# Two groups of block 0's down products by Strassen's scheme, and a scheduler that holds 16-bit products for each other

## The chip, the cores and the metric

The kernel runs on one core of a Trainium2 chip. The metric is the device time of one execution in microseconds (us). The engines are named as in the profile: PE is TensorE (matmuls), DVE is VectorE, ACT is ScalarE, POOL is GpSimd, SP is SyncE, which issues the DMAs.

## The reference

One layer of an encoder, for 2048 prompt frames and 64 frames of a running stream, 1024 channels wide. Its second half, where most of the change lies, is a gated feed-forward network (FFN):

```python
x = x + jnp.concatenate([o_delta, o_pool], axis=-1) @ w_out
h = rmsnorm(x, norm2_w)
x = x + (jax.nn.silu(h @ w_gate) * (h @ w_up)) @ w_down
```

The first half makes `o_delta`, by a gated delta rule over chunks of frames for four heads, and `o_pool`, by means over trailing windows, from one input projection.

## The kernel before, in words

**Two stages.** The first stage (0 to about 940 us) runs over four blocks of 512 frames (the first has the 64 stream frames too). Its large products, the input and output projections, are fp32r matmuls (tiles `pp`, `pz`, weights `wsp`), each done three times on operands that are split into a high and a low part. Between them stand the small products of the delta rule: 16-bit ones (`py`, `pt`, `px` and `pf` with `_p` in their names, which solve the triangular system step by step), and plain fp32 ones and transposes (`pk`, `po`, `gr`, `ptv`). The delta rule is a chain: each small product waits for ACT or DVE to copy out the one before.

The second stage is the FFN. Its 2112 frames are cut into three blocks (`b` = 0, 1, 2) of two halves of 352 columns each. The 2816 hidden channels are 22 tiles `f`, in six groups of 4, 4, 4, 4, 2, 4 (`FGROUPS`, numbered `gi` = 0 to 5).

**Gate and up** (`gate_up`, L1530). For each f, the pair of gate and up products over the two halves of the input channels is done by Strassen's scheme in the Winograd form: seven products of 12 matmuls in place of eight (PSUM tiles `px`, `py`, `pz`). The seven weight forms are `11`, `12`, `22` and the sums `S1` to `S4`. In block 0 POOL makes these sums (`wrS`), DVE and ACT split them, and they are stored to DRAM; blocks 1 and 2 load them back (`prep_strassen`, L590). The result, `hr`, is silu(gate) * up for one f.

**Down, plain** (`down`, L1577). For a group, each of 8 output tiles and each half sums 12 matmuls over four f into a PSUM tile `d`, and DVE adds it to `y`. Each `hr` must first be split into a high and a low part (tile `h`).

**Down, Strassen** (`down_strassen`, L1611, with `factors`, L1588, and `prep_down`, L624). Two f make a pair. `factors` makes seven forms of a pair (tile `hq`, sums `q` on POOL, splits on ACT and DVE). `prep_down` makes the seven weight forms for two output tiles (sums `wrda`, `wrdb` on POOL, splits `wsd`, `wsdS`). Then four steps of seven products of 6 matmuls (PSUM tiles `dx`, `dy`, `dz`) are each added to one `y`. `plain` (L512) says which groups go which way: all of block 0, and the last group of block 2, are plain; the others go by Strassen.

**Memory that ties steps together.** The split `h` of block 0 lie in six slots of two buffers with the tag `op` (`six`, L1633); the factors `hq` and the split tiles `h3l` of a last plain group use the same two buffers. `hr` has three buffers.

**What sets the order.** `order` (L516 on) lists gate-up steps `gu` and down groups `dn`: a group stands behind the gate-up step after its last f, and group 0 (`LATER`) one step later still. Weights are prepared three sets ahead (`AHEAD`). All engine calls are recorded, and `Machine.issue` (L185) then puts each engine's instructions in an order by a model of their costs. For TensorE, `pick` (L283) chooses among the ready products. Kind `r` is fp32r, all others are small. When the last product was fp32r and there are other fp32r products ready, a small product is held back until `HOLD` us after it became ready (three numbers at L1692: for boosted ones, the others, and boosted ones before a given point of the program), so that several run together.

Of the kernel before, what the change touches and what calls it, by code (L numbers as in the profile page):

```python
# [25 lines left out]
NF = 22  # L26
# [18 lines left out]
SUBS2 = ((0, N2), (N2, N2))  # L45
FGROUPS = (4, 4, 4, 4, 2, 4)

SDOWN = (1, 2)
LASTPOOLS = {3: ((0,), (1,), (2, 3))}

FW = ("11", "S1", "S2", "12", "S3", "S4", "22")
# [8 lines left out]
class Machine:  # L60
# [124 lines left out]
    def issue(self):  # L185

        ops, self.ops = self.ops, []
        wait = {e: [] for e in self.free}
        ready = {e: [] for e in self.free}
        for op in ops:  # L190
            op.left = sum(1 for p in op.preds.values() if p.start is None)
            op.start = None

        def free(op):

            for nm in op.tiles:
                if not self.tiles[nm][1]:
                    self.parked.setdefault(nm, []).append(op)
                    return serve(self.tiles[nm][0])
            heapq.heappush(wait[op.eng], (op.ready, op.order, op))  # L200

        def serve(tag):

            q = self.queue[tag]
            nm = next((nm for nm in (q if tag[1] == "mm" else list(q)[:1]) if nm in self.parked), None)
            if nm and self.slots[tag]:
                q.remove(nm)
                at, self.tiles[nm][1] = heapq.heappop(self.slots[tag]), True
                for op in self.parked.pop(nm):
                    op.ready = max(op.ready, at)  # L210
                    free(op)
                serve(tag)

        for op in ops:
            op.left = 0
            for p in op.preds.values():
                if p.start is None:
                    op.left += 1
                    p.succs.append(op)
                else:  # L220
                    op.ready = max(op.ready, self.done(p, op))

        for op in ops:
            if op.eng == "sync" and op.succs and not op.store:
                op.rank = max(op.order, min(q.order for q in op.succs))
        for op in ops:
            if not op.left:
                free(op)
        out, front = [], 0
        while len(out) < len(ops):  # L230
            best = None
            for e in self.free:
                if ready[e]:
                    t = self.free[e]
                    if e == "sync":

                        t = max(t, self.wire - (BACKLOG if ready[e][0][0] < front + AHEAD_OPS else IDLE))
                        if wait[e]:
                            t = min(t, max(self.free[e], wait[e][0][0]))
                elif wait[e]:  # L240
                    t = max(self.free[e], wait[e][0][0])
                else:
                    continue
                if best is None or t < best[0]:
                    best = (t, e)
            t, e = best
            while wait[e] and wait[e][0][0] <= t:
                op = heapq.heappop(wait[e])[2]
                heapq.heappush(ready[e], (op.rank, op.order, op))
            if e == "sync" and self.wire - (BACKLOG if ready[e][0][0] < front + AHEAD_OPS else IDLE) > t:  # L250
                continue
            if e == "tensor":
                op = self.pick(ready[e], t)
                front = max(front, op.order)
            else:
                op = heapq.heappop(ready[e])[2]
            self.run(op, t)
            out.append(op)
            for nm in op.tiles:
                t = self.tiles[nm]  # L260
                t[2] -= 1
                t[3] = max(t[3], op.start + op.lat + 0.04)
                if not t[2]:
                    heapq.heappush(self.slots[t[0]], t[3])
                    serve(t[0])
                self.early -= t[4]
                self.gone = max(self.gone, t[3] if t[4] else 0.0)
            if not self.early and self.later:
                later, self.later = self.later, {}
                for tag, n in later.items():  # L270
                    self.slots[tag] = [self.gone] * n
                    serve(tag)
            for q in op.succs:
                q.ready = max(q.ready, self.done(op, q))
                q.left -= 1
                if not q.left:
                    free(q)
        for op in out:
            name, args, kw = op.call
            getattr(getattr(self.nc, op.eng), name)(*args, **kw)  # L280
            op.call = op.preds = op.succs = None

    def pick(self, ready, t):  # L283

        others = sorted(x for x in ready if x[2].kind != "r")
        if others:
            first = others[0]
            held = self.last == "r" and len(others) < len(ready) and t < min(x[2].ready + self.hold(x) for x in others)
            if held:
                first = min(x for x in ready if x[2].kind == "r")  # L290
            ready.remove(first)
            heapq.heapify(ready)
            return first[2]
        return heapq.heappop(ready)[2]
# [67 lines left out]
def hybrid_kernel(ctx, tc, a, o):  # L362
# [140 lines left out]
    groups, f0 = [], 0  # L503
# [6 lines left out]
        return ((0,), (1,)) if (b, gi) == (NB2 - 1, len(groups) - 1) else ((0, 1),)  # L510

    def plain(b, gi):  # L512
        return b not in SDOWN or len(halves(b, gi)) > 1

    order = []
    for b in range(NB2):  # L516
        for f in range(NF):
            order.append(("gu", b, f))
            order += [("dn", b, gi) for gi, (f0, G) in enumerate(groups) if f == min(f0 + G + LATER * (gi == 0), NF - 1)]
    for op in order:  # L520
        if op[0] == "gu":
            plan.append(("gu", op[2]))
# [1007 lines left out]
    def gate_up(b, f):  # L1530
        w = weights("gu", f)
        tag = f"{b}_{f}"
        raw = f2.tile([P, 2, N2], F32, tag="hr", name=f"hr{tag}", bufs=3)

        def add(ps, nw, nh, first=False):

            for i, t in enumerate(hq[nh]):
                ks = slice(i * P, (i + 1) * P)
                for q, (wi, ai) in enumerate(((0, 0), (0, 1), (1, 0))):
                    mm(ps, w[nw][:, wi, ks], t[:, ai, :], start=first and i == q == 0, stop=i == 3 and q == 2,  # L1540
                       skip_group_check=not first)
                pump()

        def sigmoid(e, x):
            act(e, x, AF.Exp, scale=-1.0)
            act(e, e, AF.Ln, bias=onec)
            act(e, e, AF.Exp, scale=-1.0)

        def finish(i, g, u):
            e = raw[:, i]  # L1550
            tt(e, e, g, ALU.mult)
            tt(e, e, u, ALU.mult)
            if b not in SDOWN:
                split(h3t[f % 6], slice(i * N2, (i + 1) * N2), e)


        x, y, z = (psg(f"p{i}_{tag}")[:, :N2] for i in "xyz")
        add(x, "11", "11", True)
        hurry(nc.scalar.copy, g1 := tmp(f"g1_{tag}"), x)
        add(y, "S1", "T1", True)  # L1560
        hurry(nc.scalar.copy, u2 := tmp(f"u2_{tag}"), y)
        add(x, "S2", "T2")
        hurry(nc.scalar.copy, g2 := tmp(f"g2_{tag}"), x)
        add(z, "12", "21", True)
        hurry(tt, g1, z, g1, ALU.add)
        sigmoid(raw[:, 0], g1)
        add(x, "S3", "T3")
        hurry(tt, u2, x, u2, ALU.add)
        add(y, "S4", "22")
        hurry(tt, g2, y, g2, ALU.add)  # L1570
        sigmoid(raw[:, 1], g2)
        finish(1, g2, u2)
        add(x, "22", "T4")
        finish(0, g1, x)
        return raw if b in SDOWN else h3t[f % 6]

    def down(b, gi, h3, ys, which, done):  # L1577
        f0, G = groups[gi]
# [66 lines left out]
    for op in order:  # L1645
        b = op[1]
        if op[0] == "gu":
# [3 lines left out]
            if op == ("gu", 0, 2):  # L1651
                nxt = Chain(between(-1))
            h3[f] = gate_up(b, f)
            if b in SDOWN:
                gi = max(g for g, (f0, G) in enumerate(groups) if f0 <= f)
                if plain(b, gi):
                    if f == groups[gi][0] or f == groups[gi][0] + 2:
                        two = opool.tile([P, 2, 2, TB2], F32R, tag="op", name=f"h3l{f}", bufs=2)
                    for i in range(2):
                        split(two[:, f % 2], slice(i * N2, (i + 1) * N2), h3[f][:, i])  # L1660
                    h3[f] = two[:, f % 2]
                elif f % 2:
                    machine.boost = HURRY if f == NF - 1 else 0
                    h3[f] = factors(b, f, h3.pop(f - 1), h3[f])
                    machine.boost = 0
# [23 lines left out]
WSCALE, FSCALE = 2048.0, 256.0  # L1689
BOOST = 100000  # L1690

HOLD = 0.4, 3.0, 0.8  # L1692
BACKLOG, IDLE, AHEAD_OPS = 4.0, 0.0, 400

MARGIN = {"tensor": 0.25, "vector": 0.1, "scalar": 0.1, "gpsimd": 0.1, "sync": 3.0}
# [137 lines left out]
```

## Time and profile before

| what | value |
|---|---|
| median of 3 runs | 2320.13 us (2318.85 to 2321.16) |
| the profiled execution, its own time | 2319.95 us |
| its span, first to last instruction | 2318.1 us |
| first stage | 0 to 940 us |
| block 0, 1, 2 of the FFN | from 940, 1406 and 1858 us |
| TensorE busy | 2290.5 us of the span |
| DVE, ACT, POOL busy | 1685.2, 1352.2, 834.4 us |
| granted TensorE clock, mean | 0.999 |

A row of the timeline or of the chain begins with its start and its length. A row of a window gives the window, its length, and the busy time of PE, of the weight loads (PEld), DVE, ACT and POOL with their instruction counts, then the granted clock, the DMA share and GB/s. A row of a group gives output tile <- input tiles, shape, count, busy time, mean ns of one, idle time ahead. All instructions have the line of one recording helper (L280), so tiles tell them apart. A row of the waits gives the sum, how often, and the longest.

### The profile page before, as it was taken

Reading aid. Unit: us, or ns where it says so; the run is one execution under the profiler, and the core shown is the slowest. Engines: PE = TensorE matmul, PEld = TensorE weight load, DVE = VectorE, ACT = ScalarE, POOL = GpSimd, SP = SyncE. Lnnn points to the kernel's source line nnn. Section 1 sums busy time; section 2 is a strip of 40 time slices with the busy share of each in tenths; the row PEclk is TensorE's granted clock in tenths of the full one; section 3 lists DMA queues with packets and bytes.
Section 4 is the critical chain, followed back from the end, with each engine's and each line's share of the span. In section 5 each row is a group of like instructions: output and inputs, shape, how many; then the busy total and the mean of one; then the engine's idle time right before and its main releaser. Section 6 shows DMA issues by size and latency. Waiting matters only on the chain.

```text
span 2318.1 us, 41343 instructions
## 1 busy us (share of the span) xinstructions
PE 2290.5 (99%) x14614; PEld 2143.5 (92%) x14614; DVE 1685.2 (73%) x3085; ACT 1352.2 (58%) x3004; POOL 834.4 (36%) x943
## 2 busy tenths in 40 slices
PE   8999999999999999999999999999999999999998
PEld 8898898878777878999999999999999999999998
DVE  8988755673677786787657675877877878767776
ACT  6887855683768864565445465554454574454444
POOL 4424222440234350554412144643331654331312
PEclk9999999999999999999999999999999999999999
DMA  8755375545465568867645377768645586455463
GB/s 294 255 179 177 140 259 198 186 147 199 164 209 172 157 207 283 301 240 261 220 157 192 136 243 230 244 214 277 195 138 191 175 299 216 149 189 187 149 198 104
DMA packets 218751, 471.34 MB, mean 203 GB/s; under 512 B 27056, under 2 KB 85424, under 8 KB 218544
## 3 DMA queue, kind: packets, MB, share of 16 engines
q1 hardware_dynamic: 218544, 468.71, 60.0%
q8 instruction: 115, 1.88, 0.3%
q14 instruction: 92, 0.75, 0.1%
HBM read 354.81 MB, written 113.80 MB: 202 GB/s over the span
## 4 chain that ended last, share of the span: by engine, by line
PE 88%; DVE 6%; ACT 3%; DMA 1%; issue 1%; POOL 0%; SPq 0%; POOLq 0%; DVEq 0%; ACTq 0%
PE px L280 21%; PE pp L280 16%; PE pz L280 13%; PE py L280 10%; PE d L280 8%; PE dx L280 6%; PE dy L280 3%; PE pk_p L280 2%; PE pt_p L280 2%; PE dz L280 2%; PE gr_p L280 1%; DVE y L280 1%; PE py_p L280 1%; ACT E L280 1%; DVE Yqk L280 1%
## 5 line engine op out<-in xcount | busy, mean ns | idle before, releaser
L280 PE MATMUL pp<-h,wsp 128*128 128x512 f32 (+1 forms) x2480 | 558.3, 366 | 10.1 <-DVE wsp L280 9.3
L280 PEld LDWEIGHTS pp<-h,wsp 128*128 128x128 f32 x2480 | 400.6, 190 | 56.3 <-ACT wsp L280 8.7
L280 ACT CAST ws<-wr 128x512 fp32r<-128x512 f32 x198 | 122.0, 618 | 197.8 <-PE px L280 55.8
L280 DVE TENSOR_TENSOR ws<-wr,ws 128x512 fp32r<-128x512 f32 x198 | 167.0, 845 | 49.8 <-ACT ws L280 45.7
L280 PE MATMUL d<-h,wsd 128*128 128x352 f32 x1056 | 170.1, 322 | 0.0
L280 PEld LDWEIGHTS d<-h,wsd 128*128 128x128 f32 x1056 | 168.8, 188 | 0.0
L280 PE MATMUL pz<-op,wsp 128*128 128x288 f32 (+1 forms) x768 | 160.6, 352 | 0.0
L280 ACT ACTIVATE hr<-g 128x352 f32<-128x352 f32 x132 | 65.7, 498 | 135.6 <-DVE g L280 135.2
L280 PE MATMUL px<-hA,ws 128*128 128x352 f32 x792 | 143.7, 322 | 0.0
L280 PE MATMUL py<-hB,wsS 128*128 128x352 f32 x792 | 142.6, 322 | 0.0
L280 PE MATMUL pz<-hB,ws 128*128 128x352 f32 x792 | 142.1, 322 | 0.0
L280 POOL TENSOR_TENSOR wrS<-wr,wrS 128x512 f32<-128x512 f32 x44 | 63.1, 1434 | 215.5 <-DMA wrS<-in_wu_dram 117.4
L280 PE MATMUL py<-hA,wsS 128*128 128x352 f32 x792 | 140.4, 322 | 0.0
L280 ACT CAST TV_p<-pt_p 128x512 f16<-128x512 f32 x192 | 111.1, 586 | 47.9 <-PE pt_p L280 46.7
L280 PE MATMUL px<-hA,wsS 128*128 128x352 f32 x792 | 138.2, 322 | 0.5 <-ACT g L280 0.5
L280 PE MATMUL px<-hBT,ws 128*128 128x352 f32 x792 | 138.2, 323 | 0.2 <-DVE u L280 0.2
L280 PE MATMUL px<-hBT,wsS 128*128 128x352 f32 x792 | 137.7, 322 | 0.0
L280 PEld LDWEIGHTS pz<-op,wsp 128*128 128x128 f32 x768 | 121.2, 188 | 12.3
L280 PEld LDWEIGHTS px<-hA,wsS 128*128 128x128 f32 x792 | 128.7, 188 | 1.2 <-ACT g L280 1.1
L280 PEld LDWEIGHTS px<-hA,ws 128*128 128x128 f32 x792 | 129.8, 188 | 0.1
L280 PEld LDWEIGHTS py<-hB,wsS 128*128 128x128 f32 x792 | 129.6, 188 | 0.0
L280 PEld LDWEIGHTS pz<-hB,ws 128*128 128x128 f32 x792 | 129.5, 188 | 0.0
(689 smaller groups left out, 5589.4 us busy)
## 6 DMA issues: line engine op xcount, KB each, us to landing
wsS<-gS SPq DMA_DIRECT2D x176, 512.0 KB, 4.5
wsp<-wnd SPq DMA_DIRECT2D x126, 512.0 KB, 3.3
gS<-wsS SPq DMA_DIRECT2D x88, 512.0 KB, 4.4
wr<-in_wg_dram SPq DMA_DIRECT2D x132, 256.0 KB, 3.1
wnd<-wsp SPq DMA_DIRECT2D x42, 512.0 KB, 5.0
xd<-x2d SPq DMA_DIRECT2D x96, 176.0 KB, 3.3
wr<-in_wu_dram SPq DMA_DIRECT2D x66, 256.0 KB, 3.5
wrd<-in_wd_dram SPq DMA_DIRECT2D x56, 256.0 KB, 3.3
```

The costliest lines, as they stand in the source:

```text
L280: getattr(getattr(self.nc, op.eng), name)(*args, **kw)
```

## The change

Two edits. First, groups 2 and 3 of block 0 (`STR0`) go by Strassen's scheme. Only f tiles of groups 0 and 1 still use the six split slots; groups 4 and 5 split into `h3l` tiles as the last group of block 2 does. The down products of groups 1, 2 and 3 of block 0 (`LATE0`) stand one gate-up step later. Second, `pick` gets one more reason to hold small products: when a small one could go now, but another that is not ready yet will be, within `SOON` = 1.4 us (boosted) or 3.0 us (not) of the time at which the first became ready, fp32r products go first. Two of the `HOLD` times shrink.

```diff
-SDOWN = (1, 2)
+STR0 = (2, 3)
+LATE0 = (1, 2, 3)
...
-    def pick(self, ready, t):
+    def pick(self, ready, t, wait):
...
             held = self.last == "r" and len(others) < len(ready) and t < min(x[2].ready + self.hold(x) for x in others)
+            if self.last == "r" and not held and len(others) < len(ready):
+                until = min(x[2].ready + (SOON if x[0] < 0 else HOLD[1]) for x in others)
+                held = any(t < x[0] <= until and x[2].kind != "r" for x in wait)
...
-        return b not in SDOWN or len(halves(b, gi)) > 1
+        return (b == 0 and gi not in STR0) or len(halves(b, gi)) > 1
...
-            order += [("dn", b, gi) for gi, (f0, G) in enumerate(groups) if f == min(f0 + G + LATER * (gi == 0), NF - 1)]
+            order += [("dn", b, gi) for gi, (f0, G) in enumerate(groups) if f == min(f0 + G + LATER * (gi == 0 or b == 0 and gi in LATE0), NF - 1)]
...
+        gi = max(g for g, (f0, G) in enumerate(groups) if f0 <= f)
+        six = b == 0 and gi < min(STR0)
...
-            if b not in SDOWN:
+            if six:
                 split(h3t[f % 6], slice(i * N2, (i + 1) * N2), e)
...
-        return raw if b in SDOWN else h3t[f % 6]
+        return h3t[f % 6] if six else raw
...
-HOLD = 0.4, 3.0, 0.8
+HOLD = 0.3, 3.0, 0.6
+SOON = 1.4
```

TensorE in the first stage, at one place in block 2 (`p2`) of the delta rule: `pt2` and `py3` are 16-bit products of two chains, `pp2_15` and `pp2_16` fp32r projection products. Before:

```order
L280 LDWEIGHTS Yt2_p2_2_1_1941
L280 MATMUL pt2_p2_2_1_1943<-TV11_p2_2_1_1922,Yt2_p2_2_1_1941 128x128
L280 MATMUL pp2_15_0_1907<-h0_2_1398,wsp0_74_1861 128x512 x3
L280 LDWEIGHTS Wh_p2_2_0_1909
L280 MATMUL py3_p2_2_0_1945<-TV02_p2_2_0_1936,Wh_p2_2_0_1909 128x128
L280 LDWEIGHTS Wh_p2_2_0_1909
L280 MATMUL py3_p2_2_0_1945<-TV02_p2_2_0_1936,Wh_p2_2_0_1909 128x128
L280 MATMUL pp2_15_0_1907<-h1_2_1399,wsp1_74_1862 128x512 x4
```

The same place now:

```order
L281 LDWEIGHTS Yt2_p2_2_1_1941
L281 MATMUL pt2_p2_2_1_1943<-TV11_p2_2_1_1922,Yt2_p2_2_1_1941 128x128
L281 LDWEIGHTS Wh_p2_2_0_1909
L281 MATMUL py3_p2_2_0_1945<-TV02_p2_2_0_1936,Wh_p2_2_0_1909 128x128
L281 LDWEIGHTS Wh_p2_2_0_1909
L281 MATMUL py3_p2_2_0_1945<-TV02_p2_2_0_1936,Wh_p2_2_0_1909 128x128
L281 MATMUL pp2_15_0_1907<-h1_2_1399,wsp1_74_1862 128x512 x3
L281 MATMUL pp2_16_0_1914<-h0_2_1398,wsp0_75_1873 128x512 x4
```

The two 16-bit runs became one, and one stretch of fp32r products between them is gone from there.

DVE at the start of block 0's down group 2 (`y` are the sums, `d` and `dx`, `dy`, `dz` the products, `wsd` down weights, `wsS` and `ws11` gate-up weights, `h3` the split of f = 12). Before:

```order
L280 TENSOR_TENSOR y0_0_3030<-y0_0_3030,d0_2_0_0_3346 128x352
L280 TENSOR_TENSOR h3_0_2966<-hr0_12_3337,h3_0_2966 128x352 x2
L280 TENSOR_TENSOR y0_0_3030<-y0_0_3030,d0_2_0_1_3347 128x352
L280 TENSOR_TENSOR wsd_160_3357<-wrd_160_3356,wsd_160_3357 128x512
L280 TENSOR_TENSOR wsd_161_3361<-wrd_161_3360,wsd_161_3361 128x512
L280 TENSOR_TENSOR y1_0_3031<-y1_0_3031,d0_2_1_0_3350 128x352
L280 TENSOR_TENSOR y1_0_3031<-y1_0_3031,d0_2_1_1_3351 128x352
```

Now:

```order
L281 TENSOR_TENSOR y0_0_3030<-y0_0_3030,dx0_2_0_3406 128x352
L281 TENSOR_TENSOR wsdS2_156_3369<-wrdb_156_3366,wsdS2_156_3369 128x512
L281 TENSOR_TENSOR y4_0_3034<-y4_0_3034,dy0_2_0_3407 128x352
L281 TENSOR_TENSOR y0_0_3030<-y0_0_3030,dz0_2_0_3408 128x352
L281 TENSOR_TENSOR hr0_13_3386<-hr0_13_3386,g2_0_13_3392 128x352
L281 TENSOR_TENSOR y0_0_3030<-y0_0_3030,dx0_2_0_3406 128x352
L281 TENSOR_TENSOR wsd11_157_3382<-wrdt_157_3378,wsd11_157_3382 128x512
L281 TENSOR_TENSOR y0_0_3030<-y0_0_3030,dy0_2_0_3407 128x352
L281 TENSOR_TENSOR hr0_13_3386<-hr0_13_3386,u2_0_13_3391 128x352
```

The group now stands behind gate-up step 13 in place of 12, one output tile receives several additions, and splits of the next steps' weights stand between them.

More of the change, by code (lines that the diff above doesn't have):

```diff
@@ L252, in issue @@
             if e == "tensor":
-                op = self.pick(ready[e], t)
+                op = self.pick(ready[e], t, wait[e])
                 front = max(front, op.order)
@@ L1653, in hybrid_kernel @@
             h3[f] = gate_up(b, f)
-            if b in SDOWN:
-                gi = max(g for g, (f0, G) in enumerate(groups) if f0 <= f)
+            gi = max(g for g, (f0, G) in enumerate(groups) if f0 <= f)
+            if b or gi >= min(STR0):
                 if plain(b, gi):
```

## Prediction

> **What bounds the kernel now.** I read the page first: busy times, slices, granted clock.
>
> ```profile
> span 2318.1 us, 41343 instructions
> PE 2290.5 (99%) x14614; PEld 2143.5 (92%) x14614; DVE 1685.2 (73%) x3085; ACT 1352.2 (58%) x3004; POOL 834.4 (36%) x943
> ...
> PE   8999999999999999999999999999999999999998
> ...
> PEclk9999999999999999999999999999999999999999
> ```
>
> TensorE is busy in every slice and its clock is granted in full. Busy alone can deceive, since matmuls are pipelined, so the second view is the list of what TensorE itself waited for.
>
> ```profile
> PE pp L280 <- DVE wsp L280: 9.3, 2, 8.7
> PE gb_p L280 <- ACT ktl_p L280: 1.4, 2, 0.8
> PE ptv_p L280 <- DVE X_p L280: 1.4, 2, 1.2
> PE dy L280 <- DVE y L280: 0.8, 1, 0.8
> ```
>
> The largest wait, 9.3 us, is almost wholly the first weights at the start. The next are 1.4 us each. So TensorE sets the time from end to end: a matmul that goes saves its own issue interval, a change between kinds of product that goes saves what it costs, and any other engine matters only where it becomes late. Two unbroken runs in the chain that ended last give the intervals.
>
> ```profile
> 586.95 10.71 PE pp L280 x47
> ...
> 1376.00 30.64 PE d L280 x192
> ```
>
> The second is one whole plain down group of block 0: 192 matmuls of 352 columns in 30.64 us, 0.160 us each (the 322 ns that the table of groups gives for such a matmul is its length in the pipeline, not its share of the time). The first gives 10.71 / 47 = 0.228 us for a matmul of 512 columns that nothing interrupts.
>
> **Term 1, the removed matmuls.** A plain group of four f tiles is 8 output tiles x 2 halves x 4 f x 3 = 192 matmuls. By Strassen it is 4 steps x 7 products x 2 pairs x 3 = 168. All have 352 columns, so 24 go per group and 48 in two groups: 48 x 0.160 = **7.7 us**. All stand on the path, because TensorE does nothing else meanwhile. The gate and up products are the same. A down group that moves behind one more gate-up step only swaps TensorE work with TensorE work. Of the moved steps' DMAs, the 256 KB loads of down weights stay eight per group and of the same bytes (two for each of four steps in place of one for each of eight); they pass the loads of one gate-up step on SP's queue, and three weight sets are prepared ahead in both kernels, so I price this at nothing. If that cover went, it would show as a wait of a down product for its weights, one transfer long.
>
> **Term 2, fewer changes of kind in the first 940 us.** By the order of the built programs, TensorE turns back to fp32r products from products of other kinds (16-bit, plain fp32, transposes) 384 times before and 338 times after: 46 fewer. The number of products is unchanged there. The price of one is read from the timeline of TensorE.
>
> ```profile
> 418.05 1.87 PE L280 MATMUL pp<-h,wsp 128*128 128x512 f32 x7
> 419.77 0.29 PE L280 MATMUL pt_p<-Yt_p,TV_p 128*128 128x128 f16 x2
> ...
> 420.42 2.09 PE L280 MATMUL pp<-h,wsp 128*128 128x512 f32 x8
> 422.36 0.23 PE L280 MATMUL pf_p<-TV_p,Wh_p 128*128 128x128 f16 x1
> ...
> 422.89 2.31 PE L280 MATMUL pp<-h,wsp 128*128 128x512 f32 x9
> 425.05 0.62 PE L280 MATMUL px_p<-TV_p,TV1F_p 128*128 128x128 f16 x8
> ```
>
> The run of seven takes 419.77 - 418.05 = 1.72 us, against 7 x 0.228 = 1.60 unbroken: 0.12 over. Eight take 1.94 against 1.82, nine 2.16 against 2.05: 0.11 over each time. The 16-bit run between them, ten products in 422.89 - 422.36 = 0.53 us, is at its own pace. So a turn costs 0.11 us at most; some of the 46 are turns from plain fp32, which I can't isolate in clean rows and could cost nearly nothing. Ends: 46 x 0.125 = 5.8 us, and 36 turns from 16-bit (the order has 266 of these before and 230 after) at a third of it, 1.4 us. I take 36 x 0.085 = **3.0 us**, nearer to the clean rows.
>
> The new rule also delays 16-bit products, by up to 1.4 us after the first of a boosted run is ready. They feed the delta rule's chain, whose own end must not come late. In the order, the last statistics product of the last head stands 613 us of fp32r work into the program before and 622 after (each matmul counted at its interval in the trace); the output products that need that head begin at 646. So 24 of the former 33 us of cover are left, and I price this at nothing; if it were gone, each further us would be paid in full. Waits inside the stage (1.4, 1.4 and smaller ones in the list above) can grow or shrink by some 3 us with a new order, for which I take nothing.
>
> **Term 3, what the two groups load on DVE and POOL.** Here the gain can be given back. The windows are: one plain group period of block 0, one quiet Strassen period of block 1, and the three densest stretches of the second stage (columns: PE, PEld, DVE, ACT, POOL busy).
>
> ```profile
> 1208.00:1293.00 85.00, 85.00 (x533) 85.00 (x532) 53.75 (x88) 41.15 (x80) 22.66 (x16) 1.00 0.49 176
> ...
> 1676.00:1757.00 81.00, 81.00 (x507) 80.91 (x506) 57.72 (x99) 38.55 (x79) 26.45 (x28) 1.00 0.53 171
> ...
> 940.00:1021.00 81.00, 80.46 (x500) 79.85 (x500) 67.57 (x90) 57.03 (x120) 44.97 (x34) 1.00 0.84 293
> ...
> 1487.00:1568.00 81.00, 80.77 (x504) 80.48 (x504) 66.32 (x113) 45.82 (x96) 48.23 (x49) 1.00 0.69 231
> ...
> 1798.00:1879.00 81.00, 78.88 (x488) 77.78 (x487) 62.66 (x98) 51.74 (x112) 56.54 (x55) 1.00 0.62 213
> ```
>
> Block 1 loads the weight sums S1 to S4 from DRAM; block 0 makes them, with 16 additions on POOL (all 22.66 us of POOL in the plain period) and 16 more splits on DVE per group period:
>
> ```profile
> L280 DVE TENSOR_TENSOR wsS<-wrS,wsS 128x512 fp32r<-128x512 f32 x16 | 11.9, 752 | 4.2 <-ACT wsS L280 4.0
> ```
>
> So a Strassen period of block 0 should have DVE 57.7 + 11.9 = 69.6 us and POOL 26.5 + 22.7 = 49.2 us busy in about 80.7 us, 118.8 together. ACT rises far less (38.6 plus 16 casts) and is not in question. The densest stretches have 112.5, 114.6 and 119.2 together, and TensorE lost 81 less its busy time there: 0.54, 0.23 and 2.12 us. The third is a block's end, where factors are made without a gate-up step behind them; groups 2 and 3 have one, and group 1's delay gives group 2's factors the same. I take 1.0 us per group, between these rows, **2.0 us** in all, with ends of 0 and 2 x 2.12 = 4.2 us. Nothing waits behind the second group's factors: their DVE subtractions stand in the order after the last addition of group 2, and are needed only four gate-up steps later.
>
> **The sum.** The profiled execution took 2319.95 us, its span 2318.1 and 1.85 around it; the median of the runs shown is 2320.13, so 0.2 us apart. 2319.95 - 7.7 - 3.0 + 2.0 = 2311.25, rounded to **2311 us**.
>
> **Rival 1, slower: DVE and POOL saturate the port that they share.** That they exclude each other shows here:
>
> ```profile
> 1224.15 0.52 DVE L280 TENSOR_TENSOR hr<-hr,g 128x352 f32<-128x352 f32 x1
> ...
> 1228.99 0.69 DVE L280 TENSOR_TENSOR wsS<-wrS,wsS 128x512 fp32r<-128x512 f32 x1 [0.28 <-ACT wsS L280]
> ...
> 1230.09 1.29 POOL L280 TENSOR_TENSOR wrS<-wr,wrS 128x512 f32<-128x512 f32 x1 [1.76 <-DMA wrS<-in_wu_dram]
> ...
> 955.37 1.50 DVE L280 TENSOR_TENSOR hr<-hr,u 128x352 f32<-128x352 f32 x1
> ...
> 955.07 1.42 POOL L280 TENSOR_TENSOR wrS<-wr,wrS 128x512 f32<-128x512 f32 x1 [4.00 <-DMA wrS<-in_wu_dram]
> ...
> 1697.44 0.74 POOL L280 TENSOR_TENSOR wrda<-wrdt,wrdl 128x256 f32<-128x256 f32 x1 [12.45 <-DMA wrdl<-in_wd_dram]
> ...
> 1493.97 0.94 POOL L280 TENSOR_TENSOR q<-hr,hr 128x352 f32<-128x352 f32 x1
> ```
>
> A DVE operation with two SBUF inputs of 352 columns takes 0.52 us alone, and 1.50 when a POOL addition has begun 0.30 us before it; it ends 0.38 us after that addition. With the free durations, a group period holds on DVE 28 + 12 weight splits at 0.69, four half ones at 0.42 (by the slope from 0.52 to 0.69), 12 multiplies and 14 factor splits at 0.52: 42.8 us. On POOL it holds 16 at 1.29, 16 at 0.74 and 8 at 0.94: 40.0 us. That is 82.8 us against TensorE's 80.7 (four steps of 84 matmuls, and 168, at 0.160). It has two degrees. If nothing overlaps and the pair is never idle, the two groups lose 2 x 2.1 = 4.2 us where I take 2.0, and the time is 2319.95 - 10.7 + 4.2 = **2313 us**. If the pair can be kept only 90% busy, a group takes 92.0 us, two lose 22.6, and the time is 2319.95 - 10.7 + 22.6 = **2332 us**. From a loss of 7.7 us per group on ((10.7 + 4.6) / 2) the change is slower. Against the second degree: the stretch at 1798, with the same 119 us together, lost 2.1.
>
> The Trainium skill, "SBUF — State Buffer", section "SBUF: two separate sides", states the pair as an exclusive lock: whichever of a two-SBUF-input DVE operation and a GpSimd operation starts first keeps it for the whole instruction, and the other fully blocks. By that rule the sum would be the 2313 of the first degree, not 2311; the 1.50 us row agrees with it.
>
> **Rival 2, no change: the held 16-bit products make the delta rule late.** If the chain's shift of 622 - 613 = 9 us of work were paid in full at the stage's end, the time would be 2311 + 9 = 2320 us. Against it: the 24 us of fp32r work still standing between.
>
> **Rival 3, the turns cost nothing** or the new order waits elsewhere by as much: 2319.95 - 7.7 + 2.0 = 2314 us, still faster. That the edit does nothing is excluded by the order, which has the 24 fewer matmuls in each group.
>
> **How the numbers follow.** The forecast has 0.50, and the first degree of rival 1 or rival 3, which end at 2313 to 2314, have 0.20. A better case, with no loss in block 0 and the upper price of a turn, 2319.95 - 7.7 - 5.8 = 2306.5, and beyond, has 0.10. Rival 2 and a port between the two degrees, both ending within 0.2% (4.6 us, about what a measurement of this kernel can tell from no change), have 0.14. The second degree of rival 1 has 0.06. The range goes from 2306 to 2317.5: above, 2319.95 - 7.7 - 1.4 + 4.2 = 2315, and 2.5 more for waits in the first stage. So faster 0.80, same 0.14, slower 0.06.
>
> **What would show it.** In the profile after: block 0's groups 2 and 3 as 168 products on dx, dy and dz, some 26.9 us each; the first gate product of block 0 about 3 us earlier; waits of TensorE for DVE's y or hq in block 0 of a us or two. I am wrong if the first stage does not shorten, or if TensorE waits over 4 us for DVE or POOL in the stretch from group 1 to group 4.

## The result, and the profile after

| | median of the runs | range | runs |
|---|---|---|---|
| before, on the same chip | 2320.88 us | 2318.85 to 2324.13 | 21 |
| after | 2316.88 us | 2314.83 to 2320.21 | 21 |

The ratio after to before is 0.9982, with a 95% interval of 0.9977 to 0.9988. So the change takes 4.0 us off, 0.18% (0.12 to 0.23). That lies inside the range of the forecast, but it is less than half of the 9 us that were forecast, and just within the 0.2% of no change, a case that had been given a chance of 0.14. The profiled execution of the kernel after took 2314.99 us, its span 2313.2; it is one of the fastest of its 21 runs. Two single executions among the experiments below, of 4553.70 and 4901.34 us, stand far above all the others and are left out of every ratio.

The page of the kernel after, to be laid beside the first lines of the prediction:

```profile
span 2313.2 us, 41375 instructions
...
PE 2282.2 (99%) x14566; PEld 2140.7 (93%) x14566; DVE 1738.4 (75%) x3137; ACT 1360.4 (59%) x3032; POOL 898.9 (39%) x991
...
PE   8999999999999999999999999999999999999998
...
PEclk9999999999999999999999999999999999999999
```

The 48 matmuls are gone (14614 before, 14566 now), DVE has 53 us more and POOL 64 us more, and TensorE still bounds the kernel. What TensorE waited for, in the kernel after (sum, how often, longest):

```profile
PE pp L281 <- DVE wsp L281: 10.3, 3, 9.0
PE dx L281 <- DVE y L281: 2.4, 2, 1.4
PE gb_p L281 <- ACT ktl_p L281: 2.0, 5, 0.6
PE dy L281 <- DVE y L281: 0.8, 1, 0.8
```

One line of more than 1 us is new: 2.4 us in which products on `dx` waited for DVE's additions to `y`. To see in which stage the time went, the first product of block 0 and that of block 1 are looked up in TensorE's timeline (start, length). Before:

```profile
939.81 1.44 PE L280 MATMUL px<-hA,ws 128*128 128x352 f32 x8
...
1406.47 1.28 PE L280 MATMUL px<-hA,ws 128*128 128x352 f32 x7
```

After:

```profile
938.60 2.08 PE L281 MATMUL px<-hA,ws 128*128 128x352 f32 x12
...
1401.41 1.28 PE L281 MATMUL px<-hA,ws 128*128 128x352 f32 x7
```

So the first stage is 1.2 us shorter (forecast 3.0). Block 0 went from 1406.47 - 939.81 = 466.7 us to 462.8, 3.9 shorter (forecast 7.7 - 2.0 = 5.7). Blocks 1 and 2 take 2318.1 - 1406.5 = 911.6 and 2313.2 - 1401.4 = 911.8 us, the same.

The busy times of the engines in three windows of the kernel after show where in block 0 the time is lost (window, its length, PE, PEld, DVE, ACT, POOL): the period before group 2, the period of group 2, and the products of group 3.

```profile
1107.00:1190.00 83.00, 83.00 (x521) 83.00 (x520) 63.22 (x94) 40.88 (x84) 46.55 (x38) 1.00 0.55 197
1190.00:1272.00 82.00, 80.97 (x505) 80.47 (x504) 78.40 (x113) 45.70 (x93) 46.48 (x39) 1.00 0.52 180
1272.00:1315.00 43.00, 41.62 (x258) 41.07 (x257) 36.63 (x67) 18.20 (x39) 13.72 (x13) 1.00 0.38 123
```

TensorE is idle for 1.03 us in the second and 1.38 us in the third. Over the whole of block 0 its idle time rises from 0.5 to 3.0 us, which is 2.5 of the 3.8 us that block 0 falls short of 7.7; the other 1.3 us show in no view as idle time. DVE is busy for 78.4 of 82 us: it has become the engine that is nearly full. This is the first stall, in the timeline of the kernel after (start, length, then the idle time before and who ended it):

```profile
1207.01 3.15 POOL L281 TENSOR_TENSOR wrS<-wrS,wr 128x512 f32<-128x512 f32 x2 [0.25 <-DMA wr<-in_wu_dram]
...
1207.67 1.35 DVE L281 TENSOR_TENSOR ws<-wr,ws 128x512 fp32r<-128x512 f32 x1
...
1208.79 1.12 PE L281 MATMUL dx<-hq,wsd 128*128 128x352 f32 x6
...
1209.37 1.08 DVE L281 TENSOR_TENSOR wsd<-wrdl,wsd 128x256 fp32r<-128x256 f32 x1
...
1210.37 0.51 DVE L281 TENSOR_TENSOR y<-y,dx 128x352 f32<-128x352 f32 x1
...
1210.94 1.23 PE L281 MATMUL dx<-hq,wsdS 128*128 128x352 f32 x6 [1.03 <-DVE y L281]
```

Read it from below. The product at 1210.94 sums into a `dx` that DVE must first have added to `y`. Its turn was at 1208.79 + 6 x 0.160 = 1209.75, so it comes 1.19 us late. The addition itself takes 0.51 us, as always; but it starts only at 1210.37, since two weight splits stand before it on DVE. They take 1.35 and 1.08 us, where the prediction has 0.69 and, worked out from its rows, 0.42 for such splits without a POOL instruction beside them, and POOL makes two sums `wrS` from 1207.01 to 1210.16. The stall at group 3 (1277.17, 1.38 us of waiting for `y`) looks alike, except that POOL makes the sums of the down weights there (`wrda`, `wrdb`): the split of a half tile `wsd` takes 0.96 us just before it, a multiplication of `hr` 1.06.

### The profile page after: what moved, and what is told of

It reads as the page before. It is cut to its first block, busy times and chain, and to the rows that moved or that the text cites. A ratio compares the mean times of both kernels' runs of the same rounds, so it can differ in the third digit from the quotient of the medians.

```text
span 2313.2 us, 41375 instructions
## 1 busy us (share of the span) xinstructions
PE 2282.2 (99%) x14566; PEld 2140.7 (93%) x14566; DVE 1738.4 (75%) x3137; ACT 1360.4 (59%) x3032; POOL 898.9 (39%) x991
## 4 chain that ended last, share of the span: by engine, by line
PE 80%; DVE 9%; ACT 5%; issue 2%; DMA 2%; POOL 1%; SPq 0%; DVEq 0%; POOLq 0%; ACTq 0%
PE px L281 19%; PE pp L281 14%; PE pz L281 12%; PE py L281 9%; PE dx L281 7%; PE d L281 6%; PE dy L281 3%; PE dz L281 2%; PE pk_p L281 2%; PE pt_p L281 1%; DVE y L281 1%; ACT E L281 1%; PE gr_p L281 1%; DVE Yqk L281 1%; PE py_p L281 1%
## 5 line engine op out<-in xcount | busy, mean ns | idle before, releaser
L281 PE MATMUL pp<-h,wsp 128*128 128x512 f32 (+1 forms) x2480 | 544.8, 363 | 10.7 <-DVE wsp L281 10.3
L281 DVE TENSOR_TENSOR ws<-wr,ws 128x512 fp32r<-128x512 f32 x198 | 178.2, 902 | 37.5 <-ACT ws L281 34.1
L281 POOL TENSOR_TENSOR q<-hr,hr 128x352 f32<-128x352 f32 x46 | 52.4, 1139 | 227.1 <-DVE hr L281 221.8
L281 PEld LDWEIGHTS py<-hA,wsS 128*128 128x128 f32 x792 | 129.3, 188 | 0.6 <-DVE wsS L281 0.6
L281 PEld LDWEIGHTS px<-hBT,ws 128*128 128x128 f32 x792 | 128.5, 188 | 1.0 <-DVE u L281 0.5
```

## The experiments

All were timed in five rounds against the kernel before. Differences are those of the medians on the same chip; where a ratio is given, so is its interval. The ratios stand as they were recorded and are not the quotients of the medians; the two differ by up to 0.06%.

**Each half of the change alone.** The first kernel is the one before with the scheduler's edit, without the two Strassen groups.

```diff
+            if self.last == "r" and not held and len(others) < len(ready):
+                until = min(x[2].ready + (SOON if x[0] < 0 else HOLD[1]) for x in others)
+                held = any(t < x[0] <= until and x[2].kind != "r" for x in wait)
...
-HOLD = 0.4, 3.0, 0.8
+HOLD = 0.3, 3.0, 0.6
+SOON = 1.4
```

> The kernel before with the scheduler's edit alone (the added rule, SOON and the smaller HOLD times); all of block 0's down groups stay plain. Theory A (each term is worth what the profiles of before and after show): the first stage shrinks by the 1.2 us that the two profiles differ by there (939.8 to 938.6 us), because the runs of small products now wait inside themselves by what the fewer turns save; time 1 to 1.5 us below before. Rival B (the turns are worth the forecast 3 us and the profile's 1.2 us is chance of one execution): 2.5 to 3.5 us below before. Rival C (the scheduler's edit is worth nothing or costs, and the whole gain is Strassen's): within 0.5 us of before, or slower.

Measured: 2319.99 us against 2320.97, 1.0 us less; ratio 0.9996 (0.9987 to 1.0005). The second is the kernel after with the old `pick` and the old `HOLD`, so the two groups alone.

```diff
-            if self.last == "r" and not held and len(others) < len(ready):
...
-HOLD = 0.3, 3.0, 0.6
-SOON = 1.4
+HOLD = 0.4, 3.0, 0.8
```

> The changed kernel without the scheduler's edit: Strassen for groups 2 and 3 of block 0, the later down groups, the old HOLD times. Theory A: block 0 shrinks by the 3.8 us that the profiles of before and after show (466.7 to 462.8 us), since TensorE gives back about 3 us of the 7.7 in waits for DVE's additions to y; time 3 to 4.5 us below before. Rival B (nearly all of the 7.7 us arrives and the scheduler's edit costs): 6 to 7.5 us below before. Rival C (the loss in block 0 is larger in most executions than in the profiled one): 1 to 2.5 us below before. In every case the first stage ends within 0.5 us of that of before in the profile.

Measured: 2318.05 us, 2.9 less; ratio 0.9986 (0.9978 to 0.9995). The halves add up, 1.0 + 2.9 = 3.9 of 4.0, though each interval reaches some 2 us to either side. Of the 7.7 us of the removed matmuls 4.8 are lost, then (2.6 to 6.5 by the interval), where 2.0 were forecast. In its profile block 0 takes 464.4 us, 2.3 less than before.

**Without POOL's sums.** The kernel after, leaving out the sums S1 to S4 of the gate and up weights for f = 10 to 17 of block 0: the raw weights stand in for them, everything else runs.

```diff
+        if 10 <= key[1] < 18:
+            raw |= {"S3": raw["11"], "S2": raw["S1"], "S4": raw["12"]}
+        else:
...
+            gt(out=raw["S3"], in0=raw["11"], in1=raw["S1"], op=ALU.subtract)
```

> The changed kernel, leaving out POOL's sums of gate and up weights for f = 10 to 17 of block 0 (the splits then read the unsummed weights, so the work of DVE, ACT and TensorE is the same in number and shape; the sums S1 to S4 of these f are missing from the computation, in blocks 1 and 2 too). It takes some 45 us of POOL work out of the two Strassen periods of block 0. Theory A (DVE's additions to y are late because DVE and POOL shut each other out): the two waits of TensorE for DVE's y, 1.2 and 1.5 us, go, and the time falls 2.5 to 4 us below the changed kernel. Rival B (DVE has too much work of its own there, or the order of its instructions is bad): the waits stay, and the time is within 1 us of the changed kernel.

Measured: 2313.06 us, 7.9 less than before and 3.8 less than after; ratio 0.9961 (0.9947 to 0.9974). Block 0 takes 458.2 us, and this is its row for the stretch of the two groups:

```profile
1107.00:1315.00 208.00, 208.00 (x1301) 207.98 (x1300) 159.54 (x277) 107.67 (x219) 57.83 (x59) 1.00 0.52 176
```

TensorE has no idle time left there, and the waits for `y` on `dx` are gone. So it is the sums' load that takes the gain back, and the 7.7 us of the matmuls are real. This does not tell yet whether POOL is late itself or slows DVE.

**The low parts by ACT.** The kernel after, where for the same f the low parts of S1 to S4 are written by a second copy on ACT in place of DVE's subtraction (the low part is then the sum itself and not its remainder). POOL keeps its sums.

```diff
-            wsplit(t[nm], raw[nm], 512, nc.vector)
+            if nm in gsd and 10 <= key[1] < 18:
+                nc.scalar.copy(t[nm][:, 0], raw[nm])
+                nc.scalar.copy(t[nm][:, 1], raw[nm])
+            else:
+                wsplit(t[nm], raw[nm], 512, nc.vector)
```

> The kernel after, where for f = 10 to 17 of block 0 the low parts of the four weight sums S1 to S4 are written by a copy on ACT instead of a subtraction on DVE (the low part is then a copy of the sum and not its remainder, so these products are others). It takes 16 x 0.74 = 11.9 us per group period from DVE and nothing from POOL. Theory A (the sum of DVE's and POOL's exclusive time decides): the sum falls from 82.8 to about 71 us per group, and most of the loss goes: 2 to 3.5 us below the kernel after. Rival B (POOL alone is late, its sums come after they are wanted): within 1 us of the kernel after, with waits of TensorE for DVE's y still there. Rival C (ACT becomes late instead): above the kernel after, with waits of gate products for ACT's ws.

Measured: 2313.71 us, 7.2 less than before and 3.2 less than after; ratio 0.9963 (0.9950 to 0.9975). The row of the same stretch:

```profile
1107.00:1315.00 208.00, 207.58 (x1297) 207.29 (x1296) 153.89 (x244) 124.09 (x252) 104.72 (x89) 1.00 0.51 177
```

POOL is as busy as in the kernel after (104.7 us against 106.7, the sum of the three windows), and TensorE's idle time falls from 2.4 to 0.4 us. So POOL alone is not what is late: taking work from either of the two engines cures it.

**Sums moved from POOL to DVE.** If the work that excludes the other engine counts, moving a sum to DVE must help, though DVE is the fuller engine, because the same sum is shorter there. The first kernel moves the 16 half-width sums `wrda` and `wrdb` per group (the key `ds` is left to blocks 1 and 2; block 0 has one of its own).

```diff
-            parts = prep_down(*key[1:])
...
+            parts = prep_down(*key[1:], nc.gpsimd if key[0] == "ds" else nc.vector)
...
-    def prep_down(m, f0, G):
+    def prep_down(m, f0, G, eng):
...
-        gt = nc.gpsimd.tensor_tensor
+        gt = eng.tensor_tensor
```

> The kernel after, with the sums wrda and wrdb of the down weights of block 0's two Strassen groups made by DVE in place of POOL: 32 additions of 128x256. Theory A (DVE and POOL lose time to each other because their two-input instructions exclude one another, and the sum of their exclusive time decides): a half-width addition takes about 0.42 us on DVE against 0.74 on POOL, so the sum falls by 16 x 0.32 = 5 us per group, and the kernel comes 1 to 2 us below the kernel after. Rival B (DVE's own queue decides, its additions to y come late because more stands before them): DVE gets 16 x 0.42 = 6.7 us more per group, and the kernel comes 1 to 3 us above the kernel after, with more waits of TensorE's dx and dy for DVE's y.

Measured: 2315.96 us, 4.9 less than before, 0.9 below after; ratio 0.9975 (0.9965 to 0.9984), whose interval overlaps that of the kernel after. The stretch, with 1.3 us idle in place of 2.4:

```profile
1107.00:1315.00 208.00, 206.73 (x1287) 205.70 (x1287) 179.01 (x307) 106.53 (x218) 77.20 (x58) 1.00 0.51 176
```

The last kernel moves the 16 full-width sums S1 to S4 for f = 10 to 17 instead.

```diff
-        gt = nc.gpsimd.tensor_tensor
+        gt = (nc.vector if 10 <= key[1] < 18 else nc.gpsimd).tensor_tensor
         gt(out=raw["S3"], in0=raw["11"], in1=raw["S1"], op=ALU.subtract)
```

> The kernel after, with the weight sums S1 to S4 for f = 10 to 17 of block 0 made by DVE in place of POOL: 16 additions of 128x512 per group period. Theory A (what DVE and POOL exclude each other by, taken together, decides): an addition takes 0.69 us on DVE against 1.29 on POOL, so the sum falls by 9.6 us per group, nearly as far as the 11.9 that brought 3.2 us when DVE's low parts went to ACT; the kernel comes 2 to 3 us below the kernel after, and TensorE's waits for DVE's y are under 1 us. Rival B (DVE's own work decides): DVE's work at its free durations rises from 42.8 + 28 additions to y and 20 other additions from PSUM at 0.51 = 67.4 to 78.4 us of TensorE's 80.7, 97 percent, and the kernel comes 1 to 5 us above the kernel after, with longer waits for DVE's y or for DVE's ws and wsS. Should it come out below all the others that compute the same, it is the better version.

Measured: 2312.99 us (2311.69 to 2314.85, five runs) against 2321.72, 8.7 us less; ratio 0.9961 (0.9947 to 0.9974). The interval lies wholly below that of the kernel after: this is the fastest kernel of the study that computes the whole. The three windows shown above for the kernel after, now here:

```profile
1107.00:1190.00 83.00, 83.00 (x521) 83.00 (x520) 67.27 (x112) 42.27 (x85) 25.00 (x22) 1.00 0.57 197
1190.00:1272.00 82.00, 82.00 (x513) 82.00 (x513) 74.36 (x134) 48.22 (x97) 23.73 (x25) 1.00 0.52 180
1272.00:1315.00 43.00, 43.00 (x270) 43.00 (x269) 35.93 (x66) 18.80 (x40) 12.49 (x13) 1.00 0.40 129
```

DVE does 21 instructions more in the second window (134 for 113) and is busy for 4 us less. The table of DVE's groups for 1190 to 1272 us tells how. In the kernel after (count, then busy time and mean ns of one):

```profile
L281 DVE TENSOR_TENSOR wsS<-wrS,wsS 128x512 fp32r<-128x512 f32 x16 | 13.8, 888 | 0.7 <-ACT wsS L281 0.7
L281 DVE TENSOR_TENSOR ws<-wr,ws 128x512 fp32r<-128x512 f32 x12 | 13.3, 1106 | 0.0
L281 DVE TENSOR_TENSOR hq<-hr,hq 128x352 fp32r<-128x352 f32 x8 | 8.9, 1155 | 0.6 <-ACT hq L281 0.6
L281 DVE TENSOR_TENSOR y<-y,dx 128x352 f32<-128x352 f32 x16 | 8.1, 510 | 0.3 <-PE dx L281 0.3
```

With the sums on DVE:

```profile
L281 DVE TENSOR_TENSOR wsS<-wrS,wsS 128x512 fp32r<-128x512 f32 x16 | 11.2, 721 | 0.1
L281 DVE TENSOR_TENSOR ws<-wr,ws 128x512 fp32r<-128x512 f32 x12 | 9.6, 809 | 0.0
L281 DVE TENSOR_TENSOR y<-y,dx 128x352 f32<-128x352 f32 x16 | 8.1, 519 | 1.1 <-PE dx L281 0.8
L281 DVE TENSOR_TENSOR wrS<-wrS,wr 128x512 f32<-128x512 f32 x8 | 6.6, 822 | 0.1
L281 DVE TENSOR_TENSOR wrS<-wr,wrS 128x512 f32<-128x512 f32 x8 | 5.5, 686 | 0.0
L281 DVE TENSOR_TENSOR hq<-hr,hq 128x352 fp32r<-128x352 f32 x8 | 4.6, 611 | 0.0
```

DVE pays 6.6 + 5.5 = 12.1 us for the sums and gets back 2.6 on `wsS`, 3.7 on `ws` and 4.3 on `hq`, and more on smaller groups. Most of its operations with two SBUF inputs come nearer to their free durations (`hq` from 1155 to 611 ns, `wsS` from 888 to 721), though not all reach them: `ws` still takes 809 ns where 0.69 us is free. The additions to `y`, whose second input is in PSUM, take 510 and 519 ns in the two: they were not stretched, only queued.

**One group, and three.** The kernel after with only group 3 of block 0 by Strassen's scheme, and with group 1 as well.

```diff
-STR0 = (2, 3)
+STR0 = (3,)
```

> The changed kernel with Strassen for group 3 of block 0 alone (group 2 plain; 24 matmuls fewer than before in place of 48). Theory A (each group loses alike, some 2.3 of its 3.8 us): 1.0 us by the scheduler and 1.5 by the group, 2.5 us below before. Rival B (the pair DVE and POOL falls behind only in the second period, when the lead of prepared weights is used up): 4 to 4.8 us below before, so as fast as two groups or faster.

Measured for one group: 2318.49 us, 2.3 less than before; ratio 0.9986 (0.9977 to 0.9995).

```profile
1107.00:1315.00 208.00, 208.00 (x1301) 208.00 (x1300) 147.51 (x244) 99.58 (x199) 79.95 (x65) 1.00 0.51 176
```

```diff
-STR0 = (2, 3)
+STR0 = (1, 2, 3)
```

> The kernel after, with block 0's group 1 by Strassen's scheme too: 24 matmuls fewer, 3.8 us. One group by Strassen's scheme in place of two kept 2.3 us of a gain of which 1.0 is the scheduler's, so a group nets about 1.3 to 1.5 us. Theory A (each group pays alike for its DVE and POOL work): 1 to 1.5 us below the kernel after. Rival B (group 1's period is also loaded by the work that block 0 still owes at its start, so the third group loses more than its 3.8 us): the kernel is 0 to 3 us above the kernel after, with new waits of TensorE between 1060 and 1190 us.

Measured for three: 2322.55 us against 2320.89; ratio 1.0002 (0.9993 to 1.0011), so no gain over the kernel before is left, and it is about 5 us above the kernel after, more than either theory had allowed.

```profile
1107.00:1315.00 208.00, 202.84 (x1247) 199.20 (x1246) 194.72 (x293) 110.16 (x223) 116.47 (x100) 1.00 0.53 179
```

The median of the one-group kernel is near the 2.5 less that equal shares would give, but its profile shows no equal shares. Block 0 takes 463.1 us with one group, 462.8 with two and 465.9 with three, against 466.7 before. The matmuls removed are worth 3.8, 7.7 and 11.5 us; so 0.2, 3.8 and 10.7 are lost. One group is nearly free, the third costs more than it saves. That the one-group kernel does not come out lower than 2318.5 lies in blocks 1 and 2, which take 913.5 us in its profile (before: 911.6), with waits of `dy` for `y` (1.7 us) and of `px` for `u` (1.2) there. The fastest kernel above has 913.7 us there too. Why these two stretches change is not traced.

**A planner that expects late operands.** `SLACK` adds a margin to the time at which the scheduler's model takes an operand of a TensorE product of the second stage to be ready. The kernel after with three times as much:

```diff
-SLACK = 0.6
+SLACK = 1.8
```

> The changed kernel with SLACK = 1.8 in place of 0.6: the scheduler expects what DVE, ACT and POOL hand to TensorE in the FFN 1.2 us later, and puts other products between (the numbers of instructions and the first stage are the same). Theory A (in block 0 DVE's additions come late by a us here and there, by how DVE and POOL happen to meet, and TensorE's order leaves them no room): the waits for y in block 0 fall below 1 us and the time falls 1.5 to 3.5 us below the changed kernel. Rival B (the two groups are bound by the throughput of DVE and POOL together, so no order helps): within 1 us of the changed kernel, with the waits elsewhere in the two groups. Rival C (the looser order costs more in blocks 1 and 2, where products wait for nothing now): slower than the changed kernel.

Measured: 2324.88 us, 4.1 more than before, 8 more than after; ratio 1.0018 (1.0010 to 1.0027). The waits of TensorE in that kernel:

```profile
PE dz L281 <- DVE y L281: 4.3, 4, 2.4
...
PE dz L281 <- DVE hr L281: 1.7, 2, 1.2
PE py L281 <- DVE hr L281: 1.2, 1, 1.2
PE pz L281 <- ACT ws L281: 1.0, 1, 1.0
...
PE py L281 <- ACT wsS L281: 0.6, 1, 0.6
PE py L281 <- ACT u L281: 0.5, 1, 0.5
...
PE px L281 <- ACT g L281: 0.5, 1, 0.5
```

Most of the 8 us lie outside block 0. Blocks 1 and 2, whose order the margin changes too, take 918.8 us (after: 911.8), and both rows of `dz` belong there. Block 0 takes 464.0 us, 1.2 longer. In its two groups, between 1050 and 1320 us, no product waits for `y` any more; the last four rows stand there instead, gate and up products that wait 2.6 us for ACT (the 1.2 us of `py` for `hr` come ahead of both groups). So this margin moves the waits of the two groups and does not remove them. That no other order could is not shown.

**The scheduler's price, from both sides.** Three more kernels ask what a turn between kinds of product costs. First, the rule with the old `HOLD`: 330 turns into fp32r in place of 390 before and 344 with the whole edit (here turns from and to the few bf16 products are counted too; the prediction's 384 and 338 leave them out).

```diff
+                until = min(x[2].ready + (SOON if x[0] < 0 else HOLD[1]) for x in others)
...
 HOLD = 0.4, 3.0, 0.8
+SOON = 1.4
```

> The kernel before with the added rule and SOON = 1.4 alone, and the old HOLD times. By the order, TensorE returns to fp32r products from others 60 times less often than before (with the smaller HOLD times it is 46). Theory A (each turn less saves some 0.07 us, and waits inside the longer runs give part of it back): between 1 and 3 us below before, and not faster than the scheduler's whole edit by more than 1 us. Rival B (turns alone count): 4 us below before, and 1 us below the kernel with the smaller HOLD times. Rival C (holding makes the chain of the delta rule wait): slower than before.

Measured: 2319.92 us, 1.05 less than before; ratio 0.9994 (0.9986 to 1.0003). Sixty turns fewer bring no more than 46. Then the kernel before without any holding, 678 turns, and with twice the holding, 299.

```diff
-HOLD = 0.4, 3.0, 0.8
+HOLD = 0.0, 0.0, 0.0
```

> The kernel before with HOLD = 0, 0, 0 (no small product is ever held for another; block 0 plain). By the order, TensorE turns to fp32r products from others 678 times in place of 390 in the same count (288 more; of these 181 from 16-bit and 86 from plain fp32 or transposes), and it changes between 16-bit and fp32 products less often (60 + 91 in place of 108 + 165). Fitted over the stretches of the first stage of four profiles, a run of 16-bit products between fp32r ones costs 0.10 us, one of fp32 0.03, a change from 16-bit to fp32 and back 0.05. Theory A (a turn costs that, and the forecast's 3 us were lost to waits inside the longer runs): some 19 us slower than before, less a few us if waits go. Rival B (a turn costs far less in the sum, as 1.0 us for 46 turns would have it): 4 to 8 us slower than before.

Measured: 2335.65 us, 14.9 more; ratio 1.0063 (1.0051 to 1.0075). For 678 - 390 = 288 turns that is 0.052 us each, between the 19 us and the 4 to 8 us that the two theories gave.

```diff
-HOLD = 0.4, 3.0, 0.8
+HOLD = 0.8, 3.0, 1.6
```

> The kernel before with HOLD = 0.8, 3.0, 1.6 and no added rule (block 0 plain). By the order 299 turns in place of 390 (69 fewer from 16-bit products). Theory A (a turn costs 0.10 or 0.03 us, and longer runs wait inside themselves by a part of it): turns alone would give 7 us; with waits given back 2 to 5 us below before, and the waits between small products in the first stage grow in the profile. Rival B (turns cost little): within 1.5 us of before. Rival C (the delta rule's chain becomes late): slower than before, with TensorE idle near the end of the first stage.

Measured: 2340.14 us, 19.4 more; ratio 1.0080 (1.0067 to 1.0092), though it has 91 turns fewer. Two windows of that kernel, and the same two of the kernel before:

```profile
200.00:300.00 100.00, 93.66 (x619) 74.31 (x618) 75.69 (x169) 78.28 (x194) 38.66 (x55) 1.00 0.46 146
...
800.00:900.00 100.00, 95.38 (x610) 78.11 (x609) 73.85 (x144) 62.15 (x146) 41.66 (x47) 0.98 0.64 184
```

```profile
200.00:300.00 100.00, 99.15 (x680) 83.30 (x680) 78.83 (x174) 77.51 (x187) 37.64 (x55) 1.00 0.49 170
...
800.00:900.00 100.00, 98.77 (x566) 79.93 (x564) 77.76 (x137) 60.31 (x138) 36.74 (x39) 1.00 0.71 216
```

From 100 to 900 us TensorE is idle for 800 - 782.8 = 17.2 us there and 800 - 796.5 = 3.5 before. Held products make the delta rule's chain late, and TensorE runs out of ready work. This explains 13.7 of the 19.4 us; where the rest goes is not traced (the granted clock in the second window is 0.98, where it was 1.00). The kernel without holding has 795.5 us busy in the same stretch, so its 15 us are not idle time: what is left to explain them is the turns.

## Why the prediction was right in direction and wrong in size

**Term 1, the matmuls: right.** 7.7 us were forecast. When the load of DVE and POOL is relieved, block 0 gives them back: 466.7 us before, 459.5 with the sums on DVE, 459.6 with the low parts on ACT, 458.2 without the sums.

**Term 2, the turns: right in direction, its size not settled.** 3.0 us were taken; 1.0 was measured for it alone and 1.1 as the difference between the two groups alone and the whole change (2.9 and 4.0 us less than before). The interval of the first (3.0 less to 1.2 more) touches the 3.0 and holds the term's lower end, 1.4. The 0.052 us a turn of the kernel without holding would make 2.4 of 46. That some of it comes back as waits is likely, since the kernel with twice the holding shows this very loss at large, and sixty turns fewer brought no more than 46. But a single execution cannot show a loss of 1 to 2 us here: two profiles with the first stage's old order reach block 0 at 939.8 and 942.9 us, nine with the new one between 938.1 and 940.3. Leaving out TensorE's idle time, that stretch takes 924.6 and 925.9 us with the old order and 922.1 to 923.1 with the new: about 2.5 us less, near the 2.4. The idle time in it is 15.2 and 17.0 us with the old order, 16.0 to 17.4 with the new. So the turns saved somewhat less than the 3.0 forecast, and the waits, taken at nothing, may have kept a part of that.

**Term 3, the load on DVE and POOL: the step that failed.** The prediction says "I take 1.0 us per group, between these rows". Measured were 4.8 in both groups (7.7 less the 2.9 of the groups alone; 2.6 to 6.5 by its interval) and 3.8 in the profiled block 0, against 2.0. The mechanism was as described, DVE and POOL late for TensorE, in the form of late additions to `y` behind stretched weight splits; the price was too low. The error was in the choice among the three rows. The forecast for a group period was 118.8 us of DVE and POOL together; the row with the same sum (119.2) had lost 2.1 us, and it was set aside for being a block's end. Two such losses are 4.2, the upper end that the prediction gives. The period in the kernel after holds even 78.4 + 46.5 = 124.9 us in 82.

**Rival 1: its exclusion is what happened, its sum is not confirmed.** The first degree named 4.2 us, and 4.8 were measured, but that nearness is partly luck. By its sum a group period has 82.8 us of exclusive work for 80.7 us of TensorE and loses the 2.1 between them. With the down sums on DVE the same sum is 82.8 - 5.1 = 77.7 us, below TensorE's time, and nothing should have been lost; block 0 still lost 3.2 us (7.7 less the 4.5 by which it became shorter). Nor are the lengths that it adds up the time that an operation holds DVE: in the kernel with the sums on DVE, a split of 0.69 us is followed by the next operation after 0.60.

```profile
1206.84 0.69 DVE L281 TENSOR_TENSOR wsdS<-wrda,wsdS 128x512 fp32r<-128x512 f32 x1
1207.44 0.52 DVE L281 TENSOR_TENSOR y<-y,dz 128x352 f32<-128x352 f32 x1
```

The Trainium skill, "SBUF — State Buffer", section "SBUF: two separate sides", states the shared pair as a lock that is held for a whole instruction. The traces agree with that: the split that takes 0.69 us free took 1.35 beside a sum on POOL, and when the sums went from POOL to DVE, `ws` fell from 1106 to 809 ns. The second degree, 2332 us, did not come. But the third group loses 10.7 - 3.8 = 6.9 us by itself, near the 7.7 from which on the prediction had a group make the kernel slower.

**Rivals 2 and 3** did not decide. No wait of 9 us stands at the first stage's end, and the turns do cost something, as the kernel without holding shows. That the new order waits elsewhere by as much as it saves, the other half of rival 3, is not excluded: the interval of the scheduler's edit alone holds no change. Neither of the two signs by which the prediction would have called itself wrong came: the first stage did shorten, by 1.2 of the 3.0 us in the two profiles, and TensorE's waits for DVE between groups 1 and 4 were 2.4 us, not 4.

By the medians, of the 5.9 us between 2311 and 2316.88, 2.8 are term 3, 2.0 are term 2 (both uncertain by some 2 us), 0.2 are rounding, and 0.9 are the base, since the profiled execution of before (2319.95) lay below the median of its later runs (2320.88).

## What to carry to other kernels

When work is added to DVE and POOL beside a TensorE that is full, add up the free durations of those instructions that exclude each other, for one period, and compare the sum with TensorE's time. It must lie well below, and not just below: of the 7.7 us of two groups, the profiled block 0 lost 3.8 at 82.8 of 80.7 us (5.4 with the old scheduler), still 3.2 at 82.8 - 5.1 = 77.7, and 0.6 at 82.8 - 9.6 = 73.2 and at 82.8 - 11.9 = 70.9 (the low parts on ACT). A sum that POOL makes in 1.29 us and DVE in 0.69 can be worth moving to the busier engine. Of a row whose conditions match, take the price, not a mean with rows that match less.

## What the runs showed of the hardware beyond that

Idle time of TensorE in the one stretch from 1107 to 1315 us goes with the busy time of DVE and POOL together, in the rows above and two more: none at 217 us (without the sums), 227 (one group) and 239 (sums on DVE), 0.4 at 259 (low parts on ACT), 1.3 at 256 (down sums on DVE), 2.8 at 279 (the larger `SLACK`), 2.4 at 285 (after), 3.1 at 288 (the two groups alone) and 5.2 at 311 (three groups). The busy time holds the time in which one engine is blocked by the other, so this is a sign to read, not a sum to predict with.

A turn between kinds of product costs TensorE time that no view shows as idle: with 288 more of them the kernel took 14.9 us longer, and TensorE was as busy as before (795.5 of 800 us in the first stage against 796.5).
